# Gate and up weights of the experts in transfers of 1 MB, and a weight ring in two parts

## The chip, the cores and the metric

One core of a Trainium2 chip runs the kernel. The time is that of one execution on the device in microseconds (us); a version is timed several times, and the median and the extremes are given. TensorE (PE, with its weight loads as PEld), VectorE (DVE), ScalarE (ACT) and GpSimd (POOL) compute; SyncE (SP) issues nearly all transfers from HBM, each of which 16 DMA engines carry together.

## The reference

Two transformer layers of one kind run first, then one layer of a second kind, on 256 tokens of width 1024, all in float32. The second kind ends in a mixture of 32 experts, each token going to four of them:

```python
def first_block(x, ...):
    for l in range(2):
        h = x @ w_cols                                    # all input projections
        mix = concat(gla(h), rwkv(h), nsa(h)) @ w_out[l]
        x = layer_norm(alpha * x + mix)
        ffn = (silu(x @ ffn_w_gate[l]) * (x @ ffn_w_up[l])) @ ffn_w_down[l]
        x = layer_norm(alpha * x + ffn)

def second_block(x, c, ...):
    x = x + gt1 * parallel_mixer(rms_norm(x) * (1 + sc1) + sh1, ...)
    x = x + gt2 * moe_ffn(rms_norm(x) * (1 + sc2) + sh2, ...)
    return rms_norm(x, g_final)

def moe_ffn(h, ...):
    top_vals, top_idx = lax.top_k(h @ w_router + b_router, 4)
    ...
    def expert_block(xb, e):                              # the tokens of expert e
        gu = xb @ w_gu[e] + b_gu[e]                       # [1024, 2048] weights
        gate, up = minimum(gu[:, :1024], 7), clip(gu[:, 1024:], -7, 7)
        return ((up + 1) * gate * sigmoid(1.702 * gate)) @ w_down[e] + b_down[e]
```

The weights of one expert are 8 MB for gate and up (`wgu`) and 4 MB for down (`wdn`).

## The kernel before

The two layers and the mixer of the third run up to about 985 us, the experts from there to 1969 us, and a last norm follows.

**Units.** All large weights come in units of 512 KB, a tile of 128 partitions by 1024 floats (4 KB a partition). An expert has 24: eight for the first half of gate and up (stage f0), eight for the second half (f1), eight for down. `first(e, x, 0, ...)` consumes units 0 to 7, `first(e, x, 1, ...)` 8 to 15, `second(e, ...)` 16 to 23. A block is 64 tokens; `BLOCKS` gives one block to most experts, three to expert 10 and two to experts 16 and 22, which go through each of their units once per block, the last time with `first` and `second`, the other times with `more`. Which expert stands at a place of the program is decided at run time: the experts are sorted by their tokens, and SP reads their numbers with `TENSOR_LOAD`, six at a time (`who`).

**The ring.** `Ring` gives each unit a place. Its 34 places are buffers of other parts of the program that are no longer needed there, in a fixed order: three `rw2`, `rows`, `xh` and `xl` (two units each), four of `t`, four `raw`, four `hi`, four `lo`, `mh` and `ml` (two each), four more `t`, and `cst1` (two). `fill(upto)` issues loads on SP in the order of the units until `upto` have been issued. A load waits until PE has consumed the unit that held the place before. The loop over the experts calls `fill` after f0, after f1 and after the down stage, each time for the eight units that this stage has freed. Before it, the mixer loads 4, 10 and 14 units into places that are free early, and the rest follow as buffers come free. SP runs its queue strictly in order, so a load that waits holds up all behind it. Transfers signal over eight lanes, so that at most eight are outstanding.

**The layers before.** `Weights` brings the units of the layers and the mixer: `load` fills one of four `raw` buffers, `cut` splits a unit into a rounded part `hi` (ScalarE) and the rest `lo` (VectorE, some on GpSimd), and PE uses both. `prime` keeps `load` four units ahead of `cut`; a `raw` buffer is free when its `lo` is done.

Of the kernel before, what the change touches and what calls it, by code (L numbers as in the profile page):

```python
# [10 lines left out]
F32R = mybir.dt.float32r  # L11
# [9 lines left out]
P = 128  # L21
S = 256
D = 1024
KT = D // P
# [198 lines left out]
def layout(inp):  # L223
# [29 lines left out]
    o["wgu"] = np.ascontiguousarray(inp["w_gu_2"][0].reshape(NE, KT, P, 2, 2, 512).transpose(0, 4, 1, 2, 3, 5)).reshape(NE, 16, P, 1024)  # L253
# [225 lines left out]
class Weights:  # L479
# [3 lines left out]
    def __init__(self, k, units, raw_only=False):  # L483
        self.k, self.units, self.raw_only = k, units, raw_only
        self.raws, self.parts = [], []
        self.nl = self.ns = self.ng = 0
        self.ahead = RAW_BUFS
        self.share = 0

    def load(self):  # L490
        k = self.k
        src, a = self.units[self.nl]
        raw = k.t(k.wp, [P, 1024], "rw2" if self.raw_only else "raw", bufs=RW2_BUFS if self.raw_only else RAW_BUFS)
        k.nc.sync.dma_start(raw.rearrange("p (a b) -> p a b", a=a) if a else raw, src)
        self.raws.append(raw)
        self.nl += 1

    def cut(self, later=None):
        k = self.k
        raw = self.raws[self.ns]  # L500
        hi = k.t(k.wp, [P, 1024], "hi", F32R, bufs=SPL_BUFS)
        lo = k.t(k.wp, [P, 1024], "lo", F32R, bufs=SPL_BUFS)
        if later is None:
            k.split(hi, lo, raw, 4 if self.share == 4 else int(self.share > self.ns % 2))
        else:
            k.nc.scalar.copy(hi, raw)
            later.append(lambda: k.nc.vector.tensor_tensor(lo, raw, hi.bitcast(F32), op=ALU.subtract))
        a = self.units[self.ns][1]
        self.parts.append([z.rearrange("p (a b) -> p a b", a=a) if a else z for z in (hi, lo)])
        self.ns += 1  # L510

    def prime(self, loads=False, end=None, later=None):
# [7 lines left out]
        while self.nl < min(n, self.ns + self.ahead):  # L520
            self.load()
        while not loads and self.ns < min(end or n, self.ng + SPL_BUFS - 1):
            self.cut(later)
            if self.nl < min(n, self.ns + self.ahead):
                self.load()
        self.k.clk.last = last

# [1191 lines left out]
class Ring:  # L1719
# [3 lines left out]
    def __init__(self, k, slots):  # L1723
        self.k, self.slots = k, slots
        self.size = sum(s[-1] for s in slots)
        self.n = self.i = 0
        self.known = 0
        self.free, self.units = [], {}

    def fill(self, upto):  # L1730
        while self.n < min(upto, NE * UNITS):
            self.load()

    def load(self):
        k = self.k
        if not self.free:
            pool, tag, width, bufs, n = self.slots[self.i % len(self.slots)]
            self.i += 1
            t = k.t(pool, [P, width], tag, bufs=bufs)
            self.free = [t[:, i * 1024:(i + 1) * 1024] for i in range(n)]  # L1740
        w = self.free.pop(0)
        e, u = divmod(self.n, UNITS)
        self.fetch(w, u, self.who(e))
        self.units[self.n] = w
        self.n += 1

    def who(self, e):

        if e < FIXED:
            return slice(e, e + 1)  # L1750
        i = (e - FIXED) % IDS
        if not i and self.known != e:
            self.known = e
            n = min(IDS, NE - e)
            _, self.late = self.k.nc.values_load_multi_w_load_instructions(self.ids[0:1, e:e + n], engines=[mybir.EngineType.SP], min_val=0, max_val=NE - 1)
        return bass.ds(self.late[i], 1)

    def fetch(self, w, u, es):
        k, d = self.k, self.k.d
        src = d["wgu"][es, u] if u < 16 else d["wdn"][es, u - 16]  # L1760
# [8 lines left out]
def ring_slots(k, sm):  # L1769
    u4 = max(LATE_SIZES)  # L1770
    one = lambda pool, tag, bufs, times: [(pool, tag, 1024, bufs, 1)] * times
    two = lambda pool, tag, width=2048: [(pool, tag, width, 1, 2)]
    s = one(k.wp, "rw2", RW2_BUFS, RW2_BUFS) + one(k.wp, "rows", 1, 1)
    s += two(k.wp, "xh") + two(k.wp, "xl")
    s += [(sm, f"t{u4}", u4, LATE_SIZES[u4], 1)] * 4
    s += one(k.wp, "raw", RAW_BUFS, RAW_BUFS) + one(k.wp, "hi", SPL_BUFS, SPL_BUFS) + one(k.wp, "lo", SPL_BUFS, SPL_BUFS)
    s += two(k.wp, "mh") + two(k.wp, "ml")
    s += [(sm, f"t{u4}", u4, LATE_SIZES[u4], 1)] * (LATE_SIZES[u4] - 7)
    return s + two(k.c1, "cst1", CST_W)


class Second:
# [11 lines left out]
    def columns(self):  # L1794
# [3 lines left out]
        self.ring.fill(4)  # L1798
# [204 lines left out]
    def out(self):  # L2003
# [6 lines left out]
        ring.fill(10)  # L2010
# [17 lines left out]
        ring.fill(14)  # L2028
# [16 lines left out]
def second_mixer(k, ws, xt, xh, xl, mod, sm):  # L2045
    ring = Ring(k, ring_slots(k, sm))
# [190 lines left out]
def moe(k, xt, ring, r, dout):  # L2237
# [139 lines left out]
    def missing():  # L2377
# [8 lines left out]
        def one_more(e, es, b, left, v, n):  # L2386
            with k.tc.If(v > n):
                held = {}
                ring.bias(r.bg[done % 4], es)
                for i in range(3):  # L2390
                    for u in range(i * KT, i * KT + KT):
                        held[e * UNITS + u] = units[(done + 1) * UNITS - KT + u % KT]
# [29 lines left out]
    for e in range(NE):  # L2422
# [19 lines left out]
        ring.fill(e * UNITS + 8 + ring.size)  # L2442
# [6 lines left out]
        ring.fill(e * UNITS + 16 + ring.size)  # L2449
# [19 lines left out]
        ring.fill((e + 1) * UNITS + ring.size)  # L2469
# [35 lines left out]
def build(tc, d, pr, stop=None):  # L2505
    with ExitStack() as es:
# [11 lines left out]
        x0 = []  # L2518
        for hf in range(2):
            x0.append(k.t(k.wp, [P, 1024], "raw", bufs=RAW_BUFS).rearrange("p (k c) -> p k c", k=4))  # L2520
# [48 lines left out]
```

## Time and profile before

| | |
|---|---|
| median of 3 runs | 1983.0 us (1981.77 to 1983.02) |
| profiled execution | 1983.48 us, of which the span from first to last instruction is 1981.7 us |
| mean granted TensorE clock | 0.968 |
| busy in the span | PE 1845.2 us (93%), VectorE 953.5 (48%), ScalarE 536.6 (27%), GpSimd 495.1 (25%) |
| weights and other data of SP's queue | 569.68 MB, its packets 76.8% of 16 engines' span |

The span is divided in time rather than in work: up to 985 us the computing engines wait for each other, after that PE and the DMA engines alone have work to speak of. A share of the DMA engines over 1.0 in a stretch means that packets on one engine overlap.

### The profile page before, as it was taken

The page shows a single profiled execution, that of the slowest core. Times are in us where ns is not written, and L with a number is a line of the kernel's source. Part 1 is how long each engine was busy: PE and PEld are TensorE (multiplying, and loading weights), DVE is VectorE, ACT ScalarE, POOL GpSimd, SP SyncE. Part 2 cuts the span into 40 slices and gives each one's busy share as a digit, 9 for nine tenths or more (in the row PEclk, how much of TensorE's full clock was granted, in tenths as well). Part 3 has the DMA queues.
Part 4 walks back from the last instruction along what each step waited for, and adds up shares of the span by engine and source line. Part 5 has one row for each costly group of instructions (what it writes and reads, how often), then busy time and mean ns, then how long its engine had stood idle before and what let it go on. Part 6 is the DMA issues. An engine that isn't in the chain of part 4 may idle for free. (4 is left out here: it accounts for less than half of the span.)

```text
span 1981.7 us, 32453 instructions
## 1 busy us (share of the span) xinstructions
PE 1845.2 (93%) x12219; PEld 1143.0 (58%) x12219; DVE 953.5 (48%) x1705; ACT 536.6 (27%) x977; POOL 495.1 (25%) x425
## 2 busy tenths in 40 slices
PE   8989989999998999988799999999999999999996
PEld 8867889888866999877533332333333333333232
DVE  3656678667656877467532322232323332323222
ACT  4424344445333444356211110101110111111011
POOL 2435399424534698022510000000000000000000
PEclk9979999999898999989699999999999999999998
DMA  7420578744322787736799999969999999999996
GB/s 270 158 87 21 172 259 277 265 150 149 130 76 99 237 271 252 253 139 208 267 405 407 408 408 407 409 250 379 408 407 408 408 407 406 404 401 408 402 408 261
DMA packets 169047, 571.82 MB, mean 289 GB/s; under 512 B 22178, under 2 KB 31842, under 8 KB 168884
## 3 DMA queue, kind: packets, MB, share of 16 engines
q1 hardware_dynamic: 168884, 569.68, 76.8%
q8 instruction: 98, 1.61, 0.3%
q14 instruction: 65, 0.53, 0.1%
HBM read 568.54 MB, written 1.07 MB: 287 GB/s over the span
## 5 line engine op out<-in xcount | busy, mean ns | idle before, releaser
L386 PE MATMUL ps<-t,t 128*128 128x128 bf16 (+13 forms) x3912 | 454.3, 326 | 27.3 <-DVE t L319 11.7
L319 DVE TENSOR_TENSOR lo<-raw,hi 128x1024 fp32r<-128x1024 f32 x187 | 296.3, 1607 | 149.2 <-ACT hi L319 147.7
L319 ACT COPY t<-ps 128x512 f32<-128x512 f32 (+4 forms) x196 | 101.5, 526 | 830.0 <-PE ps L386 782.4
L386 PE MATMUL ps<-xh,hi 128*128 128x256 f32 x1184 | 306.6, 294 | 10.0 <-ACT hi L319 10.0
L386 PE MATMUL ps<-xh,lo 128*128 128x256 f32 x1184 | 301.6, 291 | 12.4 <-DVE lo L319 12.3
L386 PEld LDWEIGHTS ps<-t,t 32*32 32x32 f32 (+4 forms) x3000 | 180.8, 144 | 202.0 <-issue 126.2
L319 POOL TENSOR_SCALAR t<-t 128x1 f32<-128x1 f32 (+2 forms) x24 | 9.8, 409 | 1129.5 <-DVE t L319 1129.2
L319 DVE TENSOR_TENSOR t<-ps,pfm 128x512 f32<-128x512 f32 (+1 forms) x108 | 74.4, 689 | 391.2 <-PE ps L390 257.2
L319 ACT CAST hi<-raw 128x1024 fp32r<-128x1024 f32 x224 | 229.1, 1048 | 98.7 <-PE ps L386 54.0
L386 PEld LDWEIGHTS ps<-xh,lo 128*128 128x128 f32 x1184 | 235.1, 199 | 16.9 <-DVE lo L319 15.3
L386 PEld LDWEIGHTS ps<-xh,hi 128*128 128x128 f32 x1184 | 235.0, 199 | 14.7 <-ACT hi L319 10.2
L386 PE MATMUL ps<-xl,hi 128*128 128x256 f32 x1184 | 168.4, 286 | 0.0
L386 PEld LDWEIGHTS ps<-xl,hi 128*128 128x128 f32 x1184 | 155.3, 195 | 0.0
L319 DVE TENSOR_TENSOR x<-x,ps 128x512 f32<-128x512 f32 x80 | 54.3, 687 | 201.6 <-PE ps L386 201.5
L319 POOL TENSOR_TENSOR acc<-acc,ada 128x1024 f32<-128x1024 f32 x48 | 127.3, 2651 | 5.1 <-DMA acc<-bada 1.3
L319 POOL TENSOR_TENSOR lo<-raw,hi 128x1024 fp32r<-128x1024 f32 x37 | 93.1, 2517 | 124.4 <-ACT hi L319 102.3
L319 POOL TENSOR_SCALAR ada<-ada,cpar 128x1024 f32<-128x1024 f32 x48 | 113.7, 2369 | 38.0 <-DMA ada<-wada 38.0
L386 PE MATMUL ps<-hi,t 128*64 128x512 f32 x424 | 99.0, 597 | 1.7 <-DMA hi<-wgu 1.5
L386 PE MATMUL ps<-raw,t 128*64 128x512 f32 x416 | 96.5, 597 | 2.0 <-DMA raw<-wgu 1.6
L390 PE MATMUL ps<-cst,t 128*128 128x128 f32 x524 | 86.0, 283 | 12.9 <-ACT t L319 9.3
L386 PE MATMUL ps<-lo,t 128*64 128x512 f32 x416 | 96.4, 596 | 1.6 <-DMA lo<-wgu 1.5
L390 PEld LDWEIGHTS ps<-cst,t 128*128 128x128 f32 x524 | 58.8, 143 | 64.7 <-issue 35.0
(190 smaller groups left out, 2203.0 us busy)
## 6 DMA issues: line engine op xcount, KB each, us to landing
raw<-wgu SPq DMA_DIRECT2D x148, 512.0 KB, 5.7
t<-wgu SPq DMA_DIRECT2D x122, 512.0 KB, 10.1
raw<-wdn SPq DMA_DIRECT2D x76, 512.0 KB, 9.2
raw<-win SPq DMA_DIRECT2D x60, 512.0 KB, 4.3
hi<-wgu SPq DMA_DIRECT2D x60, 512.0 KB, 8.9
t<-wdn SPq DMA_DIRECT2D x58, 512.0 KB, 9.6
lo<-wgu SPq DMA_DIRECT2D x56, 512.0 KB, 10.1
ada<-wada SPq DMA_DIRECT2D x48, 512.0 KB, 4.1
```

The lines of the kernel that those rows point to most:

```text
L319: r = f(*args, **kw)
L386: self.clk.note("PE", "mm", [out, lhsT, rhs], cost, self.nc.tensor.matmul(out, lhsT, rhs, start=start, stop=stop, skip_group_check=True))
L390: self.clk.note("PE", "tr", [out, in_], 110.0, self.nc.tensor.transpose(out, in_, ident))
```

## The change

Gate and up weights are laid out in HBM so that two units lie side by side, 8 KB a partition, and one transfer of 1 MB brings both ("a two"). Down weights stay at 512 KB ("a one"). The ring is divided by the size of its places: 11 twos (`xh`, `xl`, two `raw`, four `parts`, `mh`, `ml`, `cst1`) and 12 ones (`rw2`, `rows`, the eight `t`), again 34 units. Each part has its own counter; `fill(a, b)` issues twos up to `a`, then ones up to `b`. So that the tiles have the size of a two, `raw` in `Weights` becomes two tiles of 2048 with two units each, loaded unit by unit as before but allocated in pairs, and `hi` and `lo` become halves of one tile `parts`; `room()` replaces the constant distance of four units. The mixer's early loads become 0 and 4, 2 and 6, 4 and 8. Experts of several blocks at run time that have no place of their own (`missing`) use other units' places, for as many loads as before.

```diff
-    o["wgu"] = np.ascontiguousarray(inp["w_gu_2"][0].reshape(NE, KT, P, 2, 2, 512).transpose(0, 4, 1, 2, 3, 5)).reshape(NE, 16, P, 1024)
+    o["wgu"] = np.ascontiguousarray(inp["w_gu_2"][0].reshape(NE, KT // 2, 2, P, 2, 2, 512).transpose(0, 5, 1, 3, 2, 4, 6)).reshape(NE, 8, P, 2048)
...
-        self.ahead = RAW_BUFS
         self.share = 0
 
     def load(self):
         k = self.k
         src, a = self.units[self.nl]
-        raw = k.t(k.wp, [P, 1024], "rw2" if self.raw_only else "raw", bufs=RW2_BUFS if self.raw_only else RAW_BUFS)
+        if self.raw_only:
+            raw = k.t(k.wp, [P, 1024], "rw2", bufs=RW2_BUFS)
+        else:
+            if self.nl % 2 == 0:
+                self.tile = k.t(k.wp, [P, 2048], "raw", bufs=RAW_BUFS // 2)
+            raw = self.tile[:, self.nl % 2 * 1024:(self.nl % 2 + 1) * 1024]
...
-        hi = k.t(k.wp, [P, 1024], "hi", F32R, bufs=SPL_BUFS)
-        lo = k.t(k.wp, [P, 1024], "lo", F32R, bufs=SPL_BUFS)
+        parts = k.t(k.wp, [P, 2048], "parts", F32R, bufs=SPL_BUFS)
+        hi, lo = parts[:, 0:1024], parts[:, 1024:2048]
...
-        while self.nl < min(n, self.ns + self.ahead):
+        while self.nl < min(n, self.room()):
             self.load()
         while not loads and self.ns < min(end or n, self.ng + SPL_BUFS - 1):
             self.cut(later)
-            if self.nl < min(n, self.ns + self.ahead):
+            while self.nl < min(n, self.room()):
                 self.load()
         self.k.clk.last = last
+
+    def room(self):
+
+        return self.ns // 2 * 2 + RAW_BUFS
...
-    def __init__(self, k, slots):
-        self.k, self.slots = k, slots
-        self.size = sum(s[-1] for s in slots)
-        self.n = self.i = 0
-        self.known = 0
-        self.free, self.units = [], {}
-
-    def fill(self, upto):
-        while self.n < min(upto, NE * UNITS):
-            self.load()
-
-    def load(self):
+    def __init__(self, k, twos, ones):
+        self.k, self.slots = k, (twos, ones)
+        self.size = len(twos), len(ones)
+        self.n = [0, 0]
+        self.known, self.late = FIXED, {}
+        self.units = {}
+
+    def fill(self, *upto):
+
+        for i, n in enumerate(upto):
+            while self.n[i] < min(n, NE * KT):
+                self.load(i)
+
+    def load(self, i):
         k = self.k
-        if not self.free:
-            pool, tag, width, bufs, n = self.slots[self.i % len(self.slots)]
-            self.i += 1
-            t = k.t(pool, [P, width], tag, bufs=bufs)
-            self.free = [t[:, i * 1024:(i + 1) * 1024] for i in range(n)]
-        w = self.free.pop(0)
-        e, u = divmod(self.n, UNITS)
-        self.fetch(w, u, self.who(e))
-        self.units[self.n] = w
-        self.n += 1
+        pool, tag, width, bufs = self.slots[i][self.n[i] % self.size[i]]
+        t = k.t(pool, [P, width], tag, bufs=bufs)
+        e, u = divmod(self.n[i], KT)
+        es = self.who(e)
+        if i:
+            self.units[e * UNITS + 16 + u] = w = t[:, 0:1024]
+            self.fetch(w, 16 + u, es)
+        else:
+            for j in range(2):
+                self.units[e * UNITS + 2 * u + j] = t[:, j * 1024:(j + 1) * 1024]
+            k.nc.sync.dma_start(t[:, 0:2048], k.d["wgu"][es, u].rearrange("o p c -> (o p) c"))
+        self.n[i] += 1
 
     def who(self, e):
 
         if e < FIXED:
             return slice(e, e + 1)
-        i = (e - FIXED) % IDS
-        if not i and self.known != e:
-            self.known = e
+        if self.known <= e:
             n = min(IDS, NE - e)
-            _, self.late = self.k.nc.values_load_multi_w_load_instructions(self.ids[0:1, e:e + n], engines=[mybir.EngineType.SP], min_val=0, max_val=NE - 1)
-        return bass.ds(self.late[i], 1)
+            late = self.k.nc.values_load_multi_w_load_instructions(self.ids[0:1, e:e + n], engines=[mybir.EngineType.SP], min_val=0, max_val=NE - 1)[1]
+            self.late = {x: v for x, v in self.late.items() if x >= e - 2} | {e + i: v for i, v in enumerate(late)}
+            self.known = e + n
+        return bass.ds(self.late[e], 1)
     def fetch(self, w, u, es):
         k, d = self.k, self.k.d
-        src = d["wgu"][es, u] if u < 16 else d["wdn"][es, u - 16]
+        src = d["wgu"][es, u // 2][:, :, u % 2 * 1024:(u % 2 + 1) * 1024] if u < 16 else d["wdn"][es, u - 16]
...
-    one = lambda pool, tag, bufs, times: [(pool, tag, 1024, bufs, 1)] * times
-    two = lambda pool, tag, width=2048: [(pool, tag, width, 1, 2)]
-    s = one(k.wp, "rw2", RW2_BUFS, RW2_BUFS) + one(k.wp, "rows", 1, 1)
-    s += two(k.wp, "xh") + two(k.wp, "xl")
-    s += [(sm, f"t{u4}", u4, LATE_SIZES[u4], 1)] * 4
-    s += one(k.wp, "raw", RAW_BUFS, RAW_BUFS) + one(k.wp, "hi", SPL_BUFS, SPL_BUFS) + one(k.wp, "lo", SPL_BUFS, SPL_BUFS)
-    s += two(k.wp, "mh") + two(k.wp, "ml")
-    s += [(sm, f"t{u4}", u4, LATE_SIZES[u4], 1)] * (LATE_SIZES[u4] - 7)
-    return s + two(k.c1, "cst1", CST_W)
+    late = lambda n: [(sm, f"t{u4}", u4, LATE_SIZES[u4])] * n
+    twos = [(k.wp, "xh", 2048, 1), (k.wp, "xl", 2048, 1)] + [(k.wp, "raw", 2048, RAW_BUFS // 2)] * (RAW_BUFS // 2)
+    twos += [(k.wp, "parts", 2048, SPL_BUFS)] * SPL_BUFS + [(k.wp, "mh", 2048, 1), (k.wp, "ml", 2048, 1), (k.c1, "cst1", CST_W, 1)]
+    ones = [(k.wp, "rw2", 1024, RW2_BUFS)] * RW2_BUFS + [(k.wp, "rows", 1024, 1)] + late(4) + late(LATE_SIZES[u4] - 7)
+    return twos, ones
...
-        self.ring.fill(4)
+        self.ring.fill(0, 4)
...
-        ring.fill(10)
+        ring.fill(2, 6)
...
-        ring.fill(14)
+        ring.fill(4, 8)
...
-        ring.fill(e * UNITS + 8 + ring.size)
+        ring.fill(e * KT + 4 + ring.size[0], e * KT + ring.size[1])
...
-        ring.fill(e * UNITS + 16 + ring.size)
+        ring.fill(e * KT + 8 + ring.size[0])
...
-        ring.fill((e + 1) * UNITS + ring.size)
+        ring.fill(0, (e + 1) * KT + ring.size[1])
```

The order of instructions on PE, VectorE, ScalarE and GpSimd is the same as before, apart from the names of buffers. SP's is not; here are three places of it. `wgu` are gate and up weights, `wdn` down weights.

At the start of the experts, before, SP's rows at the end of the first filling of the ring and the beginning of its second round (`cst` is the ring's last place, `rw` its first):

```order
L319 DMA cst_1673_10477<-wgu 128x1024 x2
L319 DMA rw_1674_10480<-wgu 128x1024
L319 DMA rw_1675_10482<-wgu 128x1024
L319 DMA rw_1676_10484<-wgu 128x1024
L319 DMA rows_10486<-wgu 128x1024
L319 DMA xh_10488<-wgu 128x1024 x2
L319 DMA xl_10491<-wdn 128x1024 x2
L319 DMA t_1682_10523<-wdn 128x1024
L319 DMA t_1683_10525<-wdn 128x1024
L319 DMA t_1684_10527<-wdn 128x1024
```

And now, from the last place of the twos on:

```order
L319 DMA cst_1326_10116<-wgu 128x2048
L319 DMA xh_10118<-wgu 128x2048
L319 DMA xl_10120<-wgu 128x2048
L319 DMA raw_10122<-wgu 128x2048
L319 DMA raw_10124<-wgu 128x2048
L319 DMA t_1331_10126<-wdn 128x1024
L319 DMA t_1332_10128<-wdn 128x1024
L319 DMA t_1333_10130<-wdn 128x1024
L319 DMA t_1334_10132<-wdn 128x1024
L319 DMA parts_10163<-wgu 128x2048
```

Before, the places come round in one sequence, whose units are those of need. Now the second loads of `xh`, `xl` and both `raw` stand ahead of the first loads of four `t` places; the ones of `rw` and `rows` were loaded in the mixer.

In the cycle of the experts (rows of the expert number between the loads are left out), SP before, from the last units of f1 to the next expert's first:

```order
L319 DMA t_1708_10695<-wgu 128x1024
L319 DMA t_1709_10697<-wgu 128x1024
L319 DMA t_1710_10699<-wdn 128x1024
L319 DMA t_1711_10701<-wdn 128x1024
L319 DMA cst_1714_10732<-wdn 128x1024
L319 DMA cst_1714_10732<-wdn 128x1024
L319 DMA rw_1715_10735<-wdn 128x1024
L319 DMA rw_1716_10737<-wdn 128x1024
L319 DMA rw_1717_10739<-wdn 128x1024
L319 DMA rows_10741<-wdn 128x1024
L319 DMA xh_10743<-wgu 128x1024
```

And now, the loads of the call of `fill` after f1 and then of the call after the down stage (without its last two rows):

```order
L319 DMA xl_10358<-wgu 128x2048
L319 DMA raw_10360<-wgu 128x2048
L319 DMA raw_10362<-wgu 128x2048
L319 DMA parts_10364<-wgu 128x2048
L319 DMA t_1371_10449<-wdn 128x1024
L319 DMA t_1372_10451<-wdn 128x1024
L319 DMA t_1373_10453<-wdn 128x1024
L319 DMA t_1374_10455<-wdn 128x1024
L319 DMA rw_1375_10457<-wdn 128x1024
L319 DMA rw_1376_10459<-wdn 128x1024
```

Before, the eight `wdn` units follow the `wgu` units of the same expert, and the next expert's come behind them. Now, in the loop's pass for one expert, `xl` takes the last `wgu` two of the next expert, `raw`, `raw` and `parts` the first three of the expert after it, and only then come eight ones: the last four `wdn` units of the next expert and the first four of the one after it.

In layer 0, where the output projection's units (`wo`) end and the feed-forward part's (`wgu`, here of the layer, not of the experts) begin, SP before:

```order
L319 DMA raw_2360<-wo 128x1024
L319 DMA raw_2366<-wo 128x1024
L319 DMA raw_2433<-wgu 128x1024
L319 DMA raw_2445<-wgu 128x1024
L319 DMA raw_2457<-wgu 128x1024
```

And now:

```order
L319 DMA raw_2311<-wo 128x1024 x2
L319 DMA raw_2381<-wo 128x1024
L319 DMA raw_2381<-wgu 128x1024
L319 DMA raw_2402<-wgu 128x1024 x2
L319 DMA cpar_2419<-pfm 128x256
```

Each load had a buffer of its own; now two loads go into one tile, one of them the last of `wo` and the first of `wgu`.

## Rows read from the trace of the kernel before

**Rows 1.** The page: busy time of PE, and GB/s in 40 slices.
```profile
PE 1845.2 (93%) x12219; PEld 1143.0 (58%) x12219; DVE 953.5 (48%) x1705; ACT 536.6 (27%) x977; POOL 495.1 (25%) x425
GB/s 270 158 87 21 172 259 277 265 150 149 130 76 99 237 271 252 253 139 208 267 405 407 408 408 407 409 250 379 408 407 408 408 407 406 404 401 408 402 408 261
```

**Rows 2.** Stretches of 25 us: busy us (x count) of PE, PEld, DVE, ACT, POOL; granted clock; DMA share; GB/s.
```profile
1025.00:1050.00 25.00, 25.00 (x150) 10.38 (x148) 6.34 (x12) 3.05 (x6) 0.00 (x0) 1.00 1.03 409
1175.00:1200.00 25.00, 22.55 (x136) 8.12 (x136) 6.24 (x13) 3.37 (x7) 0.00 (x0) 1.00 1.03 408
1325.00:1350.00 25.00, 24.48 (x107) 8.13 (x108) 8.09 (x17) 0.37 (x1) 0.00 (x0) 1.00 0.41 144
```

**Rows 3.** PE in order of time: starts of e10, e11 and e12.
```profile
1262.81 1.08 PE L386 MATMUL ps<-rw,t 128*64 128x512 f32 x4
1343.93 1.89 PE L386 MATMUL ps<-ml,t 128*64 128x512 f32 x8
1369.40 1.89 PE L386 MATMUL ps<-hi,t 128*64 128x512 f32 x8
```

**Rows 4.** PE in order of time: e29, and the start of e30.
```profile
1872.70 2.27 PE L386 MATMUL ps<-hi,t 128*64 128x512 f32 x8 [0.30 <-DMA hi<-wgu]
1876.44 1.08 PE L386 MATMUL ps<-hi,t 128*64 128x512 f32 x4 [0.19 <-DMA hi<-wgu]
1904.20 2.25 PE L386 MATMUL ps<-xl,t 128*64 128x512 f32 x8 [0.28 <-DMA xl<-wgu]
```

**Rows 5.** Waits of SP from 1290 to 1360: total, times, longest.
```profile
SPq L319 <- PE ps L386: 32.7, 15, 24.5
```

**Rows 6.** Waits from 0 to 1000, of SP and of PE.
```profile
SPq L319 <- DVE lo L319: 254.7, 116, 14.2
PE ps L386 <- DVE lo L319: 14.3, 14, 2.2
```

**Rows 7.** DMA in five stretches: 1360:1640, 1095.2:1095.7, 1012.3:1012.8, 500.5:503.5, 14:16.
```profile
q1 hardware_dynamic: 32557, 113.91, 102.5%
q14 instruction: 1, 0.01, 4.0%
q14 instruction: 1, 0.01, 3.9%
DMA packets 1107, 1.11 MB, mean 370 GB/s; under 512 B 38, under 2 KB 1102, under 8 KB 1107
DMA packets 203, 0.83 MB, mean 416 GB/s; under 512 B 22, under 2 KB 22, under 8 KB 203
```

**Rows 8.** Start of the experts: PE and SP in time, and a 5 us stretch.
```profile
985.46 2.80 PE L386 MATMUL ps<-rw,t 128*64 128x512 f32 x12
986.58 2.04 SPq L319 DMA_DIRECT2D rw<-wgu  x3
990.00:995.00 5.00, 5.00 (x30) 2.49 (x28) 1.07 (x6) 1.87 (x2) 0.00 (x0) 1.00 1.00 365
```

**Rows 9.** SP in order of time in e16.
```profile
1518.10 1.51 SPq L319 DMA_DIRECT2D mh<-wgu  x2
1523.40 0.87 SPq L319 DMA_DIRECT2D ml<-wgu  x2
```

**Rows 10.** Feed-forward of layer 0: SP, ScalarE; page: issues, KB, us to landing.
```profile
346.20 1.46 SPq L319 DMA_DIRECT2D raw<-wgu  x2
353.69 2.00 ACT L319 CAST hi<-raw 128x1024 fp32r<-128x1024 f32 x2
raw<-wgu SPq DMA_DIRECT2D x148, 512.0 KB, 5.7
```

**Rows 11.** Last wo units of layer 0: SP, DVE and PE in order of time.
```profile
195.65 2.57 SPq L319 DMA_DIRECT2D raw<-wo  x2
203.86 1.22 DVE L319 TENSOR_TENSOR lo<-raw,hi 128x1024 fp32r<-128x1024 f32 x1 [1.76 <-ACT hi L319]
211.13 0.50 PE L386 MATMUL ps<-lo,mh 128*128 128x512 f32 x1 [1.37 <-DVE lo L319]
```

More of the change, by code (lines that the diff above doesn't have):

```diff
@@ L2045, in second_mixer @@
 def second_mixer(k, ws, xt, xh, xl, mod, sm):
-    ring = Ring(k, ring_slots(k, sm))
+    ring = Ring(k, *ring_slots(k, sm))
     router = Router(k, xt, mod, sm)
@@ L2391, in one_more @@
                     for u in range(i * KT, i * KT + KT):
-                        held[e * UNITS + u] = units[(done + 1) * UNITS - KT + u % KT]
+                        held[e * UNITS + u] = units[done * UNITS + (10, 11, 12, 13, 14, 15, 22, 23)[u % KT]]
                         ring.fetch(held[e * UNITS + u], u, es)
@@ L2517, in build @@
         xh, xl = k.t(k.wp, [P, KT, S], "xh", F32R), k.t(k.wp, [P, KT, S], "xl", F32R)
-        x0 = []
+        x2 = k.t(k.wp, [P, 2048], "raw", bufs=RAW_BUFS // 2)
+        x0 = [x2[:, hf * 1024:(hf + 1) * 1024].rearrange("p (k c) -> p k c", k=4) for hf in range(2)]
         for hf in range(2):
-            x0.append(k.t(k.wp, [P, 1024], "raw", bufs=RAW_BUFS).rearrange("p (k c) -> p k c", k=4))
             nc.sync.dma_start(x0[hf], d["xT"].rearrange("(k p) c -> p k c", p=P)[:, hf * 4:hf * 4 + 4, :])
```

## The prediction

> **What bounds the kernel now.** I read the page first: PE is busy 93% of the span, and in the last half the DMA rate stands at 401 to 410 GB/s but for two slices and the last [rows 1]. That half, from 985 us on, is the 32 experts. In stretches of 25 us there the DMA engines are full (share 1.03, 408 GB/s) and PE is full or nearly so, except around 1300 to 1350, where the DMA falls to 0.41 [rows 2]. Two rates race, and the starts of experts give both. Paced by PE, f0 of e11 starts at 1343.93 and f0 of e12 at 1369.40: 25.5 us per expert [rows 3]. Paced by DMA, f0 of e29 starts at 1872.70 and of e30 at 1904.20: 31.5 us, and PE waits some 0.2 us for each unit [rows 4]. A unit of 512 KB at 408 GB/s is 1.285 us, an expert of 24 units 30.8 us. PE would gain 5 us per expert on the DMA; it lives on the 34 units that the ring holds when it starts. Up to e6 it loses nothing (25.00 of 25 us busy), in e7 to e9 it waits for weights (22.55) [rows 2]. Expert e10 has three blocks of tokens and takes from 1262.81 to 1343.9 [rows 3]; the ring fills, SP waits up to 24.5 us for PE, and the DMA stands still [rows 5]. There the race starts anew with a full ring; e16 and e22, two blocks each, let the DMA catch up, and PE waits again from e28 on. So PE loses time to weights in two places, the ends of the two stretches, and what delays or hastens weights shows once in each. Before 985 us the two layers and the second mixer run from a pool of four raw buffers, where SP waits for `lo` and PE for `lo` 14.3 us in all [rows 6].
>
> **The rate of 8 KB rows.** PE, VectorE, ScalarE and POOL keep their order; only SP's queue changes, so all rests on when weights land. In the stream of now a unit of 1.285 us is eight 4 KB rows on each of 16 engines, 160.6 ns a row; the profile counts the engines at 102.5% there, so a row of its counting is 164.6 ns. Two 8 KB packets seen beside the stream took 4.0% and 3.9% of 16 engines in 0.5 us, 320 and 312 ns [rows 7]. Against 2 x 164.6 the first saves 9 ns per pair, and with 8 pairs per engine 73 ns per MB (2.8%); the second, the upper bound, 17 ns, or 134 in the time of the stream (17 x 8 / 1.025). Lower bound: 1 KB rows ran at 370 GB/s [rows 7], 44.3 ns each; a line through 44.3 and 160.6 has 5.5 ns per row that does not grow with its size, so 8 rows less save 44 ns. Nothing at all, if an 8 KB row travels as two packets. I take 73, from the packet at 320, which lies nearer to the line.
> The Trainium skill (DMA: Bandwidth & Descriptors, Rules for kernel authors) wants 1 MiB or more per DMA for the best bandwidth. The trace does not show that today's 512 KB lose anything of that kind: at 408 GB/s the engines have no gap.
>
> **The start of the ring (A).** Before, 34 units are loaded when e0 starts at 985.46, SP refills slot by slot from 986.58, and the DMA is back at 365 GB/s from 990 on [rows 8]. After, 11 twos and 8 ones are loaded: 30 units. Next in the queue is a two for `xh`, which waits until PE is through two units, and four `t` slots that are free stand behind it and three more twos. PE takes about 0.9 us a unit (twelve matmuls, three units, in 2.80 [rows 8]), so the first issue is 0.9 us later, and 4 x 1.285 = 5.1 us of loading lies in the stream instead of ahead of it: **+6.0** where PE waits at the end of the first stretch.
>
> **The order (B).** Before, units come in the order of need. After, SP issues per expert four twos, four twos, eight ones, and three twos of the next expert's f0 stand ahead of the last four wdn units of this one. When PE waits for those, the DMA has carried 3 MB that could have waited: 3 x (2.57 - 0.07) = **+7.5**. It is not paid anew by each expert, since the twos are then there, but it is there at the end of each stretch.
>
> **First stretch (C).** By the last wdn of e9, 83 twos are loaded, 11 of them before the start: 72 x 73 ns = -5.3. Expert e10 starts 6.0 + 7.5 - 5.3 = +8.2 later.
>
> **Second stretch (D).** It starts when e10's wdn slots come free, with 290 units loaded, as before (99 twos, 92 ones), so A does not recur. B does: +7.5. By the last wdn of e30, 251 - 99 = 152 twos have come faster: -11.1. The DMA can't use all of it. At e16 SP now already meets the ring's end: a pair issued from 1518.10 on was through at 1519.6, the next came only at 1523.40, out of e16's last wdn [rows 9], while the stream just held. Six experts of eight twos make the DMA 48 x 73 ns = 3.5 us early there, and it meets a slot in use; likewise at e22. Of each 3.5 the eight transfers in flight may cover between all and nothing, so idle of 0 to 7.0; I take 1.6 us as covered each time, a little under half, so 2 x 1.9 = +3.8. D = 7.5 - 11.1 + 3.8 = +0.2.
>
> **The layers.** `raw` comes in pairs now, so a pair's first load waits until the `lo` of both old units is done. In the feed-forward part two loads are issued from 346.20 on, the second at 347.33; the first would come 1.1 us later and land 5.7 us after, at 353.0, and its `hi` is at 353.69 [rows 10]: hidden, and without that cover about 1 us a pair. At the last wo units of layer 0 it isn't: the second load of the window at 195.65 (197.9) would wait for the `lo` that runs 1.22 us from 203.86; its `hi` slips by 2 to 3 us, and PE, which already waits 1.37 us for `lo` at 211.13, waits 1 to 2 us more [rows 11]. Elsewhere PE's waits for `lo` measure how close the chain of load, `hi`, `lo` and matmul is: 14.3 us in all [rows 6]; were the pairs to double them it would be about +15 (14.3 and the 1 to 2 above). Nothing is the other bound. I take +2.5, near the one place that I could follow. `parts` joins `hi` and `lo`, which PE lets go of together: nothing; SP's ids and router rows move by microseconds with the pairs, beside loads that are hidden.
>
> **Sum.** 8.2 + 0.2 + 2.5 = +10.9. On the profiled execution (1983.48 us; span 1981.7) that is 1994.4, on the median of 1983.0, 0.5 lower, **1993.9**. In general, with s ns saved per MB (of 35 and more), 13.5 + 7.5 - 3.2 + 2.5 = 20.3 us, less 72 + 152 - 96 = 128 ns for each ns: +14.7 at 44, +3.1 at 134. At 73 with idle 0 it is +7.1, with idle 7.0 +14.1; at 134 with idle 0 it would be -6.5.
>
> **Rivals.**
> 1. *No rate gain.* 6.0 + 7.5 in the first stretch, 7.5 in the second, 2.5 in the layers: +23.5, **2006.5**. For it: the stream has no gaps that a larger transfer could close. Against: 320 ns for 8 KB.
> 2. *The layers cost 15 instead of 2.5*: +23.4, **2006**. For it: SP waits 254.7 us for `lo` [rows 6], and each such wait now ends one unit later. Against: the loads that I followed land before `hi` wants them, but at the one place above.
> 3. *The other side: the rate outruns the order.* What decides is the price of 1 MB under the stream. At s = 200 (442 GB/s) the first stretch is 13.5 - 14.4 = -0.9, the second 7.5 - 30.4 + 2 x (9.6 - 1.6) = -6.9, the layers +2.5: -5.3, **1977.7**. It turns at s = 159, 435 GB/s, and shows from 190 on. For it: what a transfer costs besides its rows can't be read from single packets. Against: no stretch that I read shows more than 416 GB/s, that one of 2 us [rows 7].
> The Trainium skill (DMA: Bandwidth & Descriptors, Where 436 GB/s comes from) puts the ceiling of the fabric at 435 GB/s, an estimated 2.41 us per MB. By it this rival could reach no change, not a gain; nothing here runs that fast.
> 4. *Gain and price cancel*, within 0.2% or 4 us, about what a measurement of this kernel can tell from no change: s of 127 to 190, or of 108 with nothing in the layers. **1984**.
>
> **Chances.** Main case 0.57, no gain 0.07, layers 0.06, other side 0.15, cancel 0.15; the upper bound of the saving lies in the last of these. Slower holds the first three, less 0.02 of the main case that lies under +4: faster 0.15, same 0.17, slower 0.68. The main case's own range is 1986 to 2000. The range for 8 in 10 reaches to the other side's 1978 and to 2005, just short of rivals 1 and 2.
>
> **What would show it.** Rate: stretches between 1020 and 1250 near 415 GB/s if 8 KB rows help by 73, 408 for rival 1, above 430 for rival 3. Start: PE's first waits for weights in e5, not e7. Order: in the bound experts PE waits for wdn, no longer for wgu at f0. e0's f0 starts near 988, e10's near 1273.5, e31's about as late against before. The ring's end: DMA shares under 1.0 near 1532 and 1717. The prediction is wrong if e10 starts at or before 1263, if e0 starts over 5 us late, or if what e10 loses is won back by e31.

## The result, and the profile after

| | median us | lowest to highest | ratio to before, 95% interval |
|---|---|---|---|
| before | 1982.38 | 1980.24 to 1983.02 (4 runs) | |
| after | 1998.73 | 1994.60 to 2002.39 (4 runs) | 1.0087 [1.0070, 1.0105] |

Slower by 16 us, where 10.9 was forecast. The profiled execution took 1994.6 us, with a span of 1992.8, 11.1 above the span of before. The page of after, busy time and GB/s by slices:

```profile
PE 1843.1 (92%) x12219; PEld 1149.5 (58%) x12219; DVE 951.1 (48%) x1705; ACT 536.9 (27%) x977; POOL 474.2 (24%) x425
GB/s 255 160 95 24 184 254 258 244 155 159 118 96 96 218 272 256 252 138 184 238 404 415 416 416 415 418 258 313 417 414 402 415 415 416 392 416 417 413 417 229
```

PE does the same work in the same time as in [rows 1]; the span is longer by waits. Where the queue is full the experts' weights come at 413 to 418 GB/s instead of 401 to 409. Two slices that were full before now have less, 402 and 392. Stretches of after (columns as in [rows 2]):

```profile
240.00:360.00 120.00, 106.17 (x836) 104.35 (x835) 85.48 (x71) 48.74 (x72) 88.78 (x45) 0.96 0.72 253
990.00:995.00 5.00, 5.00 (x45) 3.63 (x44) 0.95 (x7) 1.75 (x3) 0.00 (x0) 0.78 0.00 0
1025.00:1050.00 25.00, 24.84 (x156) 10.48 (x154) 7.04 (x17) 3.70 (x7) 0.01 (x1) 1.00 1.02 417
1175.00:1200.00 25.00, 20.46 (x92) 5.89 (x88) 6.24 (x16) 1.94 (x4) 0.00 (x0) 1.00 1.02 416
1535.00:1545.00 10.00, 9.65 (x40) 3.37 (x42) 2.77 (x5) 0.24 (x1) 0.00 (x0) 1.00 0.87 338
```

The DMA runs at 416 and yet PE is busy only 20.46 of 25 us from 1175 on (22.55 in [rows 2]). The last row is the ring's end at e16: a DMA share of 0.87. PE in order of time (columns as in [rows 3]): a wait in the feed-forward part, the starts of e0, e10, e11 and e30, and between them the first waits for weights in e5:

```profile
247.34 0.38 PE L386 MATMUL ps<-xh,parts 128*128 128x256 f32 x1 [4.09 <-ACT parts L319]
993.38 1.94 PE L386 MATMUL ps<-xh,t 128*64 128x512 f32 x8
1136.77 1.94 PE L386 MATMUL ps<-raw,t 128*64 128x512 f32 x8 [0.54 <-DMA raw<-wgu]
1150.56 1.08 PE L386 MATMUL ps<-t,t 128*64 128x512 f32 x4 [0.20 <-DMA t<-wdn]
1279.67 1.51 PE L386 MATMUL ps<-raw,t 128*64 128x512 f32 x6
1360.78 1.46 PE L386 MATMUL ps<-xh,t 128*64 128x512 f32 x6
1916.58 1.89 PE L386 MATMUL ps<-ml,t 128*64 128x512 f32 x8
```

Against [rows 8], [rows 3] and [rows 4], e0 starts 7.9 us later, e10 and e11 16.9 and e30 12.4. So 7.9 us are lost before the experts, 9 in the first stretch, and 4.5 are won back in the second by e30 (5.7 by the end of the span). SP in order of time shows where two of these begin, in the feed-forward part and at the start of the experts:

```profile
228.69 0.29 SPq L319 DMA_DIRECT2D acc<-bada  x1
238.36 0.35 SPq L319 DMA_DIRECT2D ada<-wada  x1
238.81 2.41 SPq L319 DMA_DIRECT2D raw<-wgu  x2
...
985.56 0.33 SPq L319 DMA_DIRECT2D cst<-wgu  x1
995.36 0.33 SPq L319 DMA_DIRECT2D xh<-wgu  x1
997.07 0.33 SPq L319 DMA_DIRECT2D xl<-wgu  x1
998.79 2.04 SPq L319 DMA_DIRECT2D raw<-wgu  x2
1000.88 1.96 SPq L319 DMA_DIRECT2D t<-wdn  x4
```

From 985.56 to 995.36 SP waits with a two for `xh`, and with it the ones for four free `t` places; they go out 5.5 us later than it. Between 990 and 995 the DMA stands at 0 GB/s. At 238.81 a pair of raw loads goes out, after a load of `ada` that waited until 238.36 for GpSimd. SP waits there in before too (9.0 us, until 242.23), but PE does not wait behind it. Now ScalarE waits for the pair:

```profile
246.24 1.04 ACT L319 CAST parts<-raw 128x1024 fp32r<-128x1024 f32 x1 [9.36 <-DMA raw<-wgu]
```

### The profile page after: what moved, and what is told of

The parts are those of the page before. It is cut to its first block, busy times and chain, and to the rows that moved or that the text cites. A ratio compares the mean times of both kernels' runs of the same rounds, so it can differ in the third digit from the quotient of the medians.

```text
span 1992.8 us, 31505 instructions
## 1 busy us (share of the span) xinstructions
PE 1843.1 (92%) x12219; PEld 1149.5 (58%) x12219; DVE 951.1 (48%) x1705; ACT 536.9 (27%) x977; POOL 474.2 (24%) x425
## 4 chain that ended last, share of the span: by engine, by line
PE 43%; DMA 19%; DVE 6%; POOL 4%; ACT 3%; issue 2%; SPq 0%; POOLq 0%; ACTq 0%; DVEq 0%
PE ps L386 41%; DMA t<-wdn 5%; DMA parts<-wgu 4%; DVE t L319 3%; DMA xh<-wgu 2%; POOL acc L319 2%; DMA rw<-wdn 2%; PE ps L390 2%; ACT t L319 2%; POOL ada L319 2%; DVE parts L319 1%; DMA rows<-wdn 1%; DMA raw<-wgu 1%; DMA mh<-wgu 1%; ACT parts L319 1%
## 5 line engine op out<-in xcount | busy, mean ns | idle before, releaser
L386 PE MATMUL ps<-t,t 32*32 32x16 f32 (+14 forms) x3856 | 436.2, 321 | 22.0 <-DVE t L319 11.3
L319 DVE TENSOR_TENSOR parts<-raw,parts 128x1024 fp32r<-128x1024 f32 x187 | 301.2, 1630 | 167.8 <-ACT parts L319 167.3
L386 PE MATMUL ps<-xh,parts 128*128 128x256 f32 x2368 | 334.5, 295 | 30.9 <-DVE parts L319 16.8
L386 PEld LDWEIGHTS ps<-xh,parts 128*128 128x128 f32 x2368 | 311.1, 201 | 41.1 <-DVE parts L319 21.0
L319 ACT CAST parts<-raw 128x1024 fp32r<-128x1024 f32 x224 | 230.9, 1049 | 128.7 <-PE ps L386 50.1
L386 PE MATMUL ps<-parts,t 128*64 128x512 f32 x840 | 193.5, 604 | 13.4 <-DMA parts<-wgu 6.9
L386 PE MATMUL ps<-xl,parts 128*128 128x256 f32 x1184 | 170.2, 288 | 0.0
L386 PEld LDWEIGHTS ps<-xl,parts 128*128 128x128 f32 x1184 | 157.3, 197 | 0.0
L319 POOL TENSOR_TENSOR acc<-acc,ada 128x1024 f32<-128x1024 f32 x48 | 121.9, 2539 | 11.9 <-DMA acc<-bada 8.3
L319 POOL TENSOR_TENSOR parts<-raw,parts 128x1024 fp32r<-128x1024 f32 x37 | 93.7, 2533 | 126.6 <-ACT parts L319 121.2
L390 PE MATMUL ps<-cst,t 128*128 128x128 f32 x524 | 85.1, 281 | 11.9 <-ACT t L319 9.3
L386 PE MATMUL ps<-parts,hh 128*128 128x512 f32 x352 | 96.1, 389 | 0.0
```

The source lines that it names most:

```text
L319: r = f(*args, **kw)
L386: self.clk.note("PE", "mm", [out, lhsT, rhs], cost, self.nc.tensor.matmul(out, lhsT, rhs, start=start, stop=stop, skip_group_check=True))
L390: self.clk.note("PE", "tr", [out, in_], 110.0, self.nc.tensor.transpose(out, in_, ident))
```

## The experiments

Each kernel is compared with the kernel before on its own chip. There are at least four chips, and the median of the kernel before on them goes from 1979.3 to 1983.2 us, so across rows the ratios compare and not the medians. For the place of a loss the table gives, from PE's rows in order of time of each profiled execution and against the one of before (985.46, 1343.93, span 1981.7): in us, the shift of e0's start, how much longer e0 to e11 takes (the first stretch), and how much longer e11 to the end of the span takes (the second).

| kernel | median, runs | ratio to before, 95% | e0 | first | second |
|---|---|---|---|---|---|
| after | 1998.73 (4) | 1.0087 [1.0070, 1.0105] | +7.9 | +8.9 | -5.7 |
| after, again | 1996.79 (6) | 1.0073 [1.0054, 1.0091] | +11.1 | +7.6 | -5.6 |
| two transfers per two | 2013.81 (5) | 1.0163 [1.0139, 1.0187] | +11.9 | +14.9 | +5.8 |
| 1 MB in 4 KB rows | 2011.38 (5) | 1.0141 [1.0122, 1.0161] | +11.4 | +12.9 | +3.6 |
| pairs alone | 1995.38 (6) | 1.0071 [1.0054, 1.0089] | +9.9 | +1.3 | -2.2 |
| ones behind in every pass | 2008.69 (5) | 1.0134 [1.0114, 1.0154] | +12.8 | +6.5 | +6.0 |
| ones first at the start | 1989.93 (6) | 1.0053 [1.0034, 1.0071] | +8.9 | +4.1 | -5.5 |
| pairs on blocks | 1989.95 (6) | 1.0050 [1.0032, 1.0069] | +2.5 | +9.3 | -6.1 |
| these three | 2004.12 (4) | 1.0117 [1.0097, 1.0137] | +8.8 | +6.9 | +5.7 |
| two passes altered | 1991.31 (10) | 1.0042 [1.0025, 1.0060] | +15.9 | +6.0 | -10.6 |
| two passes, ones first, blocks | 1979.29 (12) | 0.9996 [0.9981, 1.0011] | +13.6 | +1.2 | -10.4 |
| the same, strict order | 1982.42 (12) | 1.0008 [0.9991, 1.0025] | +7.1 | +0.7 | -9.6 |
| pairs alone, on blocks | 1987.77 (8) | 1.0036 [1.0021, 1.0050] | -1.3 | +1.3 | -2.2 |

The two kernels with "pairs alone" have the rate and the order of before in the experts, but `raw` and `parts` are places of two units in their ring too. Both show +1.3 and -2.2 there, so that much comes neither from the rate nor from the order; which part of the pairs brings it was not tried.

**After, again.**

> The changed kernel once more, beside the others. Its four times so far lie in two pairs, 1994.6 and 1995.5, 2002.0 and 2002.4. Theory (the four terms of the prediction, layers mis-sized): e0's f0 near +7.9 us against the kernel before, e10's near +17, the end near +12, so a time near 1994 to 1996; a second group near 2002 would be a property of the executions, with the same starts of experts up to the place where it differs. Rival: the slow pair is another chip, and all times of this one chip lie in one group.

Six times spread from 1991.4 to 2000.9; the two pairs of the first four were no two groups. In the two profiled executions the stretches agree within 1.3 us; e0's start doesn't (+7.9, +11.1).

**Two transfers per two, and one transfer in 4 KB rows.** The first loads the halves of a two one by one, the second takes both with one transfer from a layout in which the units lie one behind the other:

```diff
-            k.nc.sync.dma_start(t[:, 0:2048], k.d["wgu"][es, u].rearrange("o p c -> (o p) c"))
+            for j in range(2):
+                self.fetch(self.units[e * UNITS + 2 * u + j], 2 * u + j, es)
...
+            k.nc.sync.dma_start(t[:, 0:2048].rearrange("p (j c) -> p j c", j=2), k.d["wgu"][es, u].rearrange("o j p c -> (o p) j c"))
```

> The changed kernel with the same two-part ring and the same order, but each two brought by two transfers of 512 KB with 4 KB rows. Theory (the order and the start cost time, the rate of 8 KB rows gives some back): the rate falls from 416 to 408 GB/s in the expert part, the first stretch loses 72 x 0.079 = 5.7 us more, e10 starts near +22.5 against the kernel before, and the second stretch 152 x 0.079 = 12 less the 4.4 us of idle at the ring's end, some 7.6 more: time about 13 us above the changed kernel, near 2008. Rival (PE loses because a unit counts as landed only with its whole MB): the changed kernel's waits shrink by 0.6 us per two that PE waits for, and this kernel is 3 to 8 us below the changed one, near 1989.

> The changed kernel with one transfer of 1 MB per two as there, but with its two units laid out one behind the other in HBM, so that rows are of 4 KB. Theory (the row sets the rate): 408 to 410 GB/s in the expert part, time within 3 us of the kernel with two transfers per two, near 2008. Rival (the size of the transfer sets it, by fewer closing writes or fewer transfers in the queues): 416 GB/s and a time within 3 us of the changed kernel, near 1995.

The packets of 1150 to 1250 us, of two transfers per two, then of one in 4 KB rows, then of after:

```profile
DMA packets 11624, 40.83 MB, mean 408 GB/s; under 512 B 1675, under 2 KB 1675, under 8 KB 11619
```

```profile
DMA packets 11239, 40.82 MB, mean 408 GB/s; under 512 B 1291, under 2 KB 1291, under 8 KB 11234
```

```profile
DMA packets 8259, 41.57 MB, mean 416 GB/s; under 512 B 1427, under 2 KB 1427, under 8 KB 4959
```

The row sets the rate; the size of the transfer gives at most the 2.4 us between the two medians, whose intervals overlap. Without the row's gain the changed order costs +14.9 and +5.8 with two transfers, +12.9 and +3.6 with one; less the +1.3 and -2.2 above, that is 11.6 to 13.6 and 5.8 to 8.0. The prediction had 13.5 for A and B and 7.5 for B alone. That PE loses by waiting for whole MBs fell: at the same rate the two halves, which PE waits for one by one (some 0.2 us before each four matmuls), were no faster than the whole.

**Pairs alone.** The kernel before with `Weights` of after, and its ring's `raw`, `hi` and `lo` places as twos in the old order of need:

```diff
-    s += one(k.wp, "raw", RAW_BUFS, RAW_BUFS) + one(k.wp, "hi", SPL_BUFS, SPL_BUFS) + one(k.wp, "lo", SPL_BUFS, SPL_BUFS)
+    s += [(k.wp, "raw", 2048, RAW_BUFS // 2, 2)] * (RAW_BUFS // 2) + [(k.wp, "parts", 2048, SPL_BUFS, 2)] * SPL_BUFS
```

> The kernel before, with its ring and its order of need (units of 512 KB), and of the change only the pairs of raw tiles and the joined parts. Theory (all of e0's delay comes from the pairs, which put raw loads behind loads of ada that wait for GpSimd): e0's f0 at +7 to +9 us against the kernel before, no further shift up to e10 and at the end, time near 1990.5. Rival (the prediction's 2.5 us for the layers, the rest from the mixer's early loads in two parts): e0's f0 at +2 to +3, time near 1985.

1995.38 us, 12.2 above the kernel before and 1.4 below the changed kernel on the same chip (the last is within the noise). Most of what the change costs is in the layers, and comes with the pairs alone. One stretch of its feed-forward part of layer 0, and the start of its e0:

```profile
240.00:360.00 120.00, 104.15 (x812) 101.93 (x811) 84.44 (x69) 48.19 (x70) 92.16 (x43) 0.96 0.70 248
```

```profile
995.37 2.80 PE L386 MATMUL ps<-rw,t 128*64 128x512 f32 x12
```

**Pairs on blocks.** A block of the feed-forward part uses two units, then a load of `ada` is issued. In layer 0 `wgu` begins with unit 35, so pairs straddle two blocks; in layer 1 with unit 136, and they don't. The edit leaves the last `wo` unit alone in its tile:

```diff
-            if self.nl % 2 == 0:
+            s = self.place(self.nl)
+            if s % 2 == 0:
...
-        return self.ns // 2 * 2 + RAW_BUFS
+        return self.place(self.ns) // 2 * 2 + RAW_BUFS
+
+    def place(self, i):
+        return i + sum(i >= w for w in (35, 136))
```

> The changed kernel, with the last wo unit of each layer alone in its raw tile, so that the pairs of wgu units in layer 0 are those that one block of the feed-forward part uses, as they already are in layer 1; ring and experts unchanged. Theory (in layer 0 pairs straddle two blocks, so that a pair's first load comes behind a load of ada that waits for GpSimd, 7 to 10 us late at units 42, 56 and 70; in layer 1, where pairs fall on blocks, nothing is lost): e0's f0 at 0 to +3 us against the kernel before instead of +8 to +11, time 7 to 9 us below the changed kernel, near 1988. Rival (half as many free tiles make every pair late, wherever its border falls): e0's f0 stays at +7 or more.

> The kernel before with pairs of raw tiles and joined parts, as in the run on the pairs alone, but with the last wo unit of each layer alone in its tile. Theory (only pairs across two blocks of the feed-forward part cost): e0's f0 at -2 to +3 us against the kernel before, where the pairs alone had +9.9, and a time of 1981 to 1986, about 10 below that of the pairs alone. Rival (the pairs cost in the mixers and layer 1 as well, and what the aligned kernel showed at e0 was one lucky execution): e0 at +5 or more, time above 1988.

From 240 to 360 us PE is busy 112.74 us in the changed kernel with pairs on blocks (106.17 in after above), and with the pairs alone on blocks:

```profile
240.00:360.00 120.00, 113.64 (x932) 111.97 (x931) 94.51 (x78) 52.73 (x77) 116.65 (x48) 1.00 0.79 272
```

```profile
984.13 2.37 PE L386 MATMUL ps<-rw,t 128*64 128x512 f32 x10
```

Over the kernels: 104 to 109 us with straddling pairs in eight of them, 110.6 to 113.6 on blocks in five, before 113.6. PE's matmuls come in one order in all kernels, so each can be set against its like in before. From 245 to 250 us of before all eight kernels with straddling pairs fall 4.4 to 7.4 us further behind, and none of the five on blocks does. The matmul that waited 4.09 us at 247.34 above starts without a wait in the changed kernel with pairs on blocks:

```profile
245.37 2.08 PE L386 MATMUL ps<-xh,parts 128*128 128x256 f32 x16
```

So this place is shown. But against before on their own chips the medians fall less than e0's start does: with all of the change from +13.6 to +10.6 us, which is within the noise, and with the pairs alone from +12.2 to +6.8, still 1.0036 of before. The profiled execution of the latter, at 1981.27, is the fastest of its eight and shows no loss; in three other kernels on blocks e0 is 7 to 14 us late. Part of that lies with TensorE's clock and not with waits. In the kernel with two passes altered, ones first and pairs on blocks, whose e0 is 13.6 us late, PE is as busy from 560 to 580 us as before, but with 116 matmuls instead of 174, at a granted clock of 0.66 instead of 0.97, and falls 4.5 us further behind; before, then this kernel:

```profile
560.00:580.00 20.00, 18.31 (x174) 13.50 (x166) 10.52 (x41) 6.91 (x35) 10.53 (x30) 0.97 0.43 133
560.00:580.00 20.00, 18.14 (x116) 14.21 (x116) 9.72 (x37) 5.97 (x23) 5.23 (x10) 0.66 0.32 106
```

What brings the clock down there, and what the pairs cost besides, stays open.

**Ones first at the start.** One line ahead of the loop over the experts:

```diff
+    ring.fill(11, 12)
     for e in range(NE):
```

> The changed kernel, with the four free t places loaded with wdn ones before the first two that waits for PE; nothing else. Theory (term A: 30 instead of 34 units are ahead when e0 starts, 5.1 us of the 6.0): e10 starts 5 to 6 us earlier against e0 than in the changed kernel (+2.5 to +4 instead of +7.6 to +9), the second stretch is unchanged, and the time is 5 to 6 us below the changed kernel, near 1991. Rival (the four ones only push the waiting twos back in the queue, since the DMA was already short of nothing before 990): within 2 us of the changed kernel.

SP in order of time: the four ones go out before the two that waits.

```profile
987.66 2.23 SPq L319 DMA_DIRECT2D t<-wdn  x4
989.94 0.48 SPq L319 DMA_DIRECT2D pfm<-bgu  x1
996.34 0.33 SPq L319 DMA_DIRECT2D xh<-wgu  x1
```

The first stretch takes 4.1 us more than before instead of 7.6, 8.9 and 9.3 in the three kernels without this edit: 3.5 to 5.2 less, for four units of 1.285 us. The second is unchanged. (By the medians on their own chips the gain is 3.0 us, within the noise.)

**The order.** In every pass the three twos go behind the last four ones of the next expert:

```diff
-        ring.fill(e * KT + 8 + ring.size[0])
+        ring.fill(e * KT + 5 + ring.size[0])
...
-        ring.fill(0, (e + 1) * KT + ring.size[1])
+        ring.fill(0, e * KT + 4 + ring.size[1])
+        ring.fill(e * KT + 8 + ring.size[0], (e + 1) * KT + ring.size[1])
```

> The changed kernel, but the three twos of the expert after next are issued behind the last four wdn ones of the next expert instead of ahead of them (order of need); nothing else. Theory (term B: 3 MB too early cost 7.5 us at the end of each stretch): from e0 to e10 the start slips by about +1 us instead of the +7.6 to +9 of the changed kernel, by the end it is another 12 us earlier than at e11, against the kernel before; in all some 14 us below the changed kernel, near 1982. Rival (PE pays for the four places filled too late, A, and for waits on whole MBs, the order is free since the twos are needed soon anyway): within 3 us of the changed kernel.

It gains 1 to 3 us in the first stretch and loses some 12 in the second. By the order of the queue, places of twos that are free now wait behind ones whose places aren't, so that the ring holds up to six units less. At e16 the DMA idles longer than in after, whose shares in these stretches are 0.87 and 1.03:

```profile
1535.00:1545.00 10.00, 9.48 (x42) 3.12 (x38) 4.64 (x11) 0.79 (x2) 0.00 (x0) 1.00 0.69 285
1545.00:1555.00 10.00, 10.00 (x47) 3.36 (x48) 3.53 (x8) 0.00 (x0) 0.00 (x0) 1.00 0.75 252
```

PE runs dry already in e15 and e21, where it falls 4.6 and 3.9 us behind. With all three edits the second stretch is as bad:

> The three edits together: order of need, ones first at the start, wgu pairs on blocks. Theory (the terms add): e0's f0 at 0 to +3 us against the kernel before, e10 at -4 to 0, the end at -10 to -17, time 1966 to 1974, about 25 below the changed kernel and 10 to 16 below the kernel before. Rival (the gains overlap, since the DMA meets the full ring at e16 and e22 when it is ahead): e10 as said, but no gain between e11 and the end, time near 1982.

The theory of additive terms fell here: the same order that is early at the end of a stretch is what keeps the ring full in its middle. So two further kernels change it only where a stretch ends, in the passes of e8 and e29 (`e in (8, 29)` chooses the 5 above, else 8):

> The changed kernel, with two passes of the expert loop altered: in those for e8 and e29 the last four wdn ones of the next expert (e9, e30) are issued ahead of the three twos of the one after it (e10, e31). All other passes are as in the changed kernel, so the ring keeps its depth. Theory (B is the 3 MB ahead of the last wdn that PE waits for, 5 to 9 us of it as measured so far): e9's down stage ends 5 to 8 us earlier against e0, e10 starts near +1 to +4 against e0's shift instead of +7.6 to +9, the three twos land while PE prepares e10 and it does not wait at f0; the end gains the same once more: time 10 to 15 us below the changed kernel, near 1985. Rival (the wait only moves, as in the kernel in order of need: PE then waits for the twos at f0 of e10 and e31): e10's f0 takes 10 to 12 us instead of 7.1, and the time is within 3 us of the changed kernel.

> The same two passes altered, with the ones first at the start and the wgu pairs on blocks. Theory (the terms add where they lie in different places): e0's f0 near +2.5 us against the kernel before, e10 near -1 to +1, from e11 to the end another 10 us or more gained: time 1968 to 1975, below the kernel before by 0.3 to 0.7%. Rival (the altered passes give nothing): e10 near +7, the end near +2, time near 1984.

The second stretch gains 4 to 5 us more, of B's 7.5. The first gains 2 to 3: e9's down stage no longer waits, but its f0 and f1 do (8.6 us each instead of 7.1), since the first four ones of e9, 4 x 1.285 = 5.1 us, still go ahead of most of e9's own twos. Holding those back as well:

> As the kernel with ones first at the start, wgu pairs on blocks and two altered passes, but with strict order of need in the two experts ahead of each end (e8 and e9, e29 and e30): the first four wdn ones of e9 and of e30 are held back too, behind all their twos. Theory (with only the last four held, the four others, 4 x 1.285 = 5.1 us, still stood ahead of the twos that PE waits for at f1, so that 2.4 of B's 7.5 came back in the first stretch and 4.9 in the second): e9's f0 and f1 wait less, e10 starts 3 to 5 us earlier against e0 than there (-2 to -4), the end gains 2 to 5 more, time 5 to 9 us below that kernel, near 1972. Rival (holding back slots idles the DMA while PE is in f1, as in the kernel in order of need at e16): a DMA share below 1.0 in e8 or e29, and no gain.

e9 waits nowhere now, and e10 starts 2.2 us earlier against e0 than before; but then it waits for a two that has become late, in PE's order of time:

```profile
1275.79 1.94 PE L386 MATMUL ps<-parts,t 128*64 128x512 f32 x8 [2.69 <-DMA parts<-wgu]
```

The two stretches together are as they were. From e0 to the end both last versions are some 9 us faster than before in their profiled executions (1.2 - 10.4 and 0.7 - 9.6), but their e0 starts 13.6 and 7.1 us late. No version beats the kernel before: 0.9996 and 1.0008, both intervals with 1 in them.

## Why the prediction was right, and where its steps failed

The direction and the range held, and so did the parts of the mechanism in the experts: DMA and PE race through two stretches, and an order that carries weights too early costs at the ends. But the sizes of the parts were wrong. The experts were to give 8.4 of the 10.9 us; they give 2 to 4, and most of the loss is in the layers, where 2.5 was taken. That the span of the profiled execution grew by 11.1 us, next to the 10.9 forecast, is luck: the layers came out 5.4 us above their term and the second stretch 5.9 below its own. By the prediction's own sign, e0 over 5 us late, it was wrong there (7.9 and 11.1).

- **Rate.** 73 ns per MB was near: an expert has 8 MB of gate and up, and 12.58 MB take 30.25 us at 416 GB/s instead of 30.84 at 408, 74 ns per MB. In the stream from 1150 to 1250 us the 8 KB packets take 315 ns on average and those of 4 KB 163, so the two single witnesses, 320 and 312, lay on either side. (The working divides the upper bound by 1.025 and not the 73; divided, it is 72.) Rivals 1 and 3 are out, and rival 4 too: 1.0070 to 1.0105 is clear of no change.
- **Start (A).** +6.0 forecast; its larger part, 5.1, measured 3.5 to 5.2, and SP's rows show the mechanism.
- **First stretch.** +8.2 forecast for e10 against e0; measured 7.6 to 9.3, or 6.3 to 8.0 above the pairs alone.
- **Second stretch (D).** +0.2 forecast, -5.5 to -6.1 measured; against the pairs alone -3.3 to -3.9. The idle at the ring's end was as taken: the two slices at 402 and 392 against 416 are 49.8 x 14/416 + 49.8 x 24/416 = 4.6 us, for 3.8. B without the row's gain was 5.8 to 8.0. The gain of the rows is then 9 to 12, where 11.1 - 3.8 = 7.3 was taken; so part of the idle seems to have cost nothing. Which part isn't settled. One thing the sum did not hold: without the gain PE waits for weights in the middle of the stretch too. With two transfers per two it falls 2.4 us behind in e15 and 1.8 in e21; with 8 KB rows in neither.
- **The layers.** This term was mis-sized, and at the wrong place. "I take +2.5, near the one place that I could follow", the last wo units: there the changed kernel is ahead. The pairs alone cost 12.2 us by their median. In the profiled executions it arises in layer 0's feed-forward part, some 45 us further on: after is 4.9 us ahead of before at 243 us of before and 6.2 behind at 360. "Hidden" was worked out there from one place at which both loads of a pair go out behind the same `ada`; which units make a pair against which make a block was not looked at, though SP's order shows it. The bound of +15 held this. Rival 2, with 15 in the layers, was nearest in this term, but its time of 2006 was not reached, since the second stretch won back 5.7 us where +0.2 was taken.
- **Sum.** 8.4 for the experts and 2.5 for the layers were forecast. By the medians on one chip it is 12.2 with the pairs alone and 13.6 with all, a difference within the noise. By the stretches of the profiled executions the experts give 2 to 3 us, or 3 to 4 against the pairs alone, since the second wins back most of what the first loses.
- **What would show it.** PE waits first in e5, as said. It waits for wdn (1150.56) and for wgu (1136.77), not for wdn alone. The DMA share falls under 1.0 at the ring's end, as said (0.87 from 1535 to 1545, 0.86 from 1715 to 1725). e0 started at 993.38, not near 988, and e31, which was to be as late as e10, is 12.1 us late where e10 is 16.9.

The Trainium skill (DMA: Bandwidth & Descriptors, Rules for kernel authors) asks for at least 1 MiB per DMA for the best bandwidth. Here 1 MB in 4 KB rows ran at the 408 GB/s of 512 KB transfers; what raised the rate to 416 was the row of 8 KB.

## What to carry to other kernels

Larger transfers into a ring change two things besides their rate: the size of a place, which couples loads that were independent, and the order of the queue. Cost both against the queue that the loads share: here a gain of 8 GB/s was worth 4 to 7 us in one stretch and 9 to 12 in the other, and at one place loads issued behind one that waits for another engine cost 4 to 7 us. Before pairing buffers, look at which loads fall into one pair and what is issued between them. And where a queue is strictly in order, an order that is early for the last consumer may be what keeps the ring full for the others: try it at the ends alone.

## What was not expected of the hardware

- Rows, not transfers: 408 GB/s with 512 KB and with 1 MB in 4 KB rows, 416 with 8 KB rows, at DMA shares of 1.03 and 1.02, so the engines had no idle time to speak of in either case.
- A wait of PE can cost more than itself in the layers. In after the granted clock from 332 to 350 us is 0.81, a stretch in which PE waits 3.1 us for `parts`; in before it was 1.00 with waits of 1.4 us. From 335 to 350 us of before, after falls 4.5 us further behind, 1.7 by the longer waits; the rest goes with matmuls at the lower of the clock's two levels, 1.2 GHz. It is not so each time: in the kernel with ones first at the start PE waits 4.4 us in this stretch at a clock of 1.00. The stretch in after:

```profile
332.00:350.00 18.00, 14.90 (x100) 14.50 (x100) 10.70 (x9) 6.09 (x9) 15.57 (x8) 0.81 0.82 291
```

- Executions of one kernel spread by 5 to 15 us here (1974.5 to 1987.9 for one of twelve runs), and what varies in the profiled ones is e0's start, not the experts: with the same layers, e0 began between 2.5 and 13.6 us late in four kernels.
